# A hybrid encoder with normalised inputs: scale and offset applied per feature after the transpose, and a residual normed a second time

## The chip, the cores and the metric

The kernel runs on one core of a Trainium2 chip. The metric is device time in microseconds (us) of one execution of the program; lower is better. The engines are named as the profile names them: PE (TensorE matmul) and PEld (its weight loads), DVE (VectorE), ACT (ScalarE), POOL (GpSimd), SP (SyncE, which issues DMAs).

## The reference, cut to what matters

Sequence 256, width 2048, two layers, float32, one batch.

```python
x = layer_norm(x, ln_emb_g, ln_emb_b)
for l in range(2):
    u, g_ssm, q, k, v, g_attn = split(x @ w_in[l])        # w_in: 2048 x 6144
    y = ssm_d * u + s5_scan(forward) + s5_scan(reverse)   # 64 groups, 64 complex states
    y = gelu(y);  y = y * sigmoid(y @ w_glu[l] + b_glu);  y_ssm = y * silu(g_ssm)
    o = diff_attention(rotary(q), rotary(k), v, lam)      # 8 heads, two softmax maps each
    y_attn = rms_norm(o, attn_norm_g) * (1 - lambda_init) * silu(g_attn)
    x = layer_norm(ALPHA * x + concat(y_ssm, y_attn) @ w_out[l], ln_g[l], ln_b[l])
```

`layer_norm` works over the 2048 features of a token: `(x - mean) * rsqrt(var + eps) * g + b`, with `g` and `b` one number for each feature.

## The kernel before, in words

All large products run as three fp32r matmuls (`mm3`, L168 to L170): a number is split into a high part and a rest (`wh`/`wl` for weights, `xh`/`xl` for inputs, written hi and lo below), and hi·hi, hi·lo and lo·hi are added. Weights come from HBM in blocks of 512 rows by 256 columns (`load`, `raw`, L149, four buffers), each split by ACT (`wh`, L162) and DVE (`wl`, L164), two blocks ahead of their use. One block makes 24 matmuls of 256 columns.

A layer goes through: input projection (24 column blocks of four weight blocks), attention heads, the attention half of the output projection (8 column blocks `cb` of two weight blocks, L943 to L951), the GLU (L960 on), the other half of the output projection (L976 on), and the norm. The last column blocks of that half ("late") are computed for tokens 0 to 127 (`i=0`) and then for tokens 128 to 255 (`i=1`), so that the norm of `i=0` runs under the matmuls of `i=1`.

The norm, `ln_finish`, works on `r`, with tokens on partitions, in the memory of the tile `H` (which the scan uses between its start and `ssm_out`); `gt` and `bt`, also in `H`, hold `g` and `b` copied to all 128 partitions by broadcast loads (`load_gb`, 256 KB each). For a piece of `nk` blocks of 128 features it runs two DVE instructions:

```python
V.scalar_tensor_tensor(r[:, i, cs], r[:, i, cs], mv[:, 0:1], gt[:, cs], sub, mult)   # L229
last = V.scalar_tensor_tensor(r[:, i, cs], r[:, i, cs], rstd, bt[:, cs], mult, add)  # L235
```

then `trans` transposes it on PE (L248), ACT evicts the hi part (`xh`, L252) and DVE makes the lo part (`xl`, L253). `rstd` comes from two POOL instructions (L223 add, L224 power). The normed `r` is stored to `xres` in DRAM, and `xr` (L946, two buffers, shared with the attention's `q` and `k`) reads it back in the attention half of the output projection, where L951 makes `part_r = ALPHA * xr + acc`. The other half adds its sums to `part_r` into `r` (L985, L1007).

Side work (state tables, the scan's input, scan and output, heads, stores) is written as generators called lanes. After each weight block `side` gives them a budget of DVE time by their declared costs and gaps in steps, so the program order is fixed by that plan; `finish` runs a lane to its end. The compiler's scheduler then orders each engine's queue from this order with its own model of times: an instruction that it takes to be ready may stand ahead of earlier ones, loads above all. On the chip each queue is in order. `after(ins)` keeps an instruction behind `ins` in its queue.

Of the kernel before, what the change touches and what calls it, by code (L numbers as in the profile page):

```python
# [14 lines left out]
D = 2048  # L15
# [16 lines left out]
LAST_PIECES = (6,5,5)  # L32
# [7 lines left out]
HEAD_HOPS = (1,1,2,2,2,3)  # L40


@with_exitstack
def kernel(
# [45 lines left out]


# [14 lines left out]
    xv = x[0].rearrange("(k j) d -> j k d", j=4)  # L106
    ov = out[0].rearrange("(k j) d -> j k d", j=4)
# [33 lines left out]
    newest = [None]  # L141

    def load(i):
# [4 lines left out]
        raw = T([128, KT, 256], "raw", RAW_BUFS)  # L148
        newest[0] = SY.dma_start(  # L149
# [5 lines left out]
    def do_split(i, wh=None, wl=None, behind=None):  # L155
# [6 lines left out]
        A.copy(wh, raw)  # L162
        with after(behind):
            V.tensor_tensor(wl, raw, wh.bitcast(F32), sub)  # L164
# [35 lines left out]
    def ln_stats(r, i, c, st):  # L200
        V.bn_stats(st[:, i, c, :], r[:, i, c * 256:(c + 1) * 256])
# [3 lines left out]
    def store_x():  # L205
        yield 0.0, STORE_HOP
        n = 0
        while n < 9:
            if stores:
                SY.dma_start(*stores.pop(0))  # L210
                n += 1
            yield 0.0, 1

    def ln_finish(r, gt, bt, st, dst, box, ahead):


        pool = [None]

        def moments(i):
            mv = T([128, 2], "mv", 2)  # L220
            V.bn_aggr(mv, st[:, i].rearrange("p c s -> p (c s)"))
            rstd = T([128, 1], "rstd", 2)
            GP.tensor_scalar(rstd, mv[:, 1:2], EPS, None, add)  # L223
            pool[0] = GP.tensor_tensor(rstd, rstd, mhalf[:, 0:1], ALU.pow).ins  # L224
            return mv, rstd
# [5 lines left out]
        def norm(i, k0, nk, mv, rstd):  # L231
            cs = slice(k0 * 128, (k0 + nk) * 128)
            if dst is None or i == 0:
                centre(i, k0, nk, mv)
            last = V.scalar_tensor_tensor(r[:, i, cs], r[:, i, cs], rstd, bt[:, cs], mult, add)  # L235
            if dst is None:
                stores.append((xres[128 * i:128 * i + 128, cs], r[:, i, cs]))
            else:
                for j in range(2):
                    SY.dma_start(dst[2 * i + j][:, cs], r[64 * j:64 * j + 64, i, cs])  # L240
            return last.ins

        def trans(k0, nk, i0, ni):

            t = ss_bank([128, nk, 128 * ni])
            for k in range(nk):
                for i in range(ni):
# [829 lines left out]
```

## Time and profile before

| what | us |
|---|---|
| runs: median of 3 (lowest to highest) | 1003.33 (999.39 to 1005.35) |
| profiled execution, time | 1002.55 |
| profiled execution, span | 1000.8 |
| PE busy | 955.8 (96%) |
| DVE busy | 780.3 (78%) |
| ACT busy | 576.0 (58%) |
| POOL busy | 71.7 (7%) |

The span runs from the first to the last instruction; the execution's time is 1.75 us more. A busy time is the time in which an engine had at least one instruction in work; what PE lacks to the span is 45.0 us. DMA moved 177.76 MB, at a mean of 178 GB/s.

### The profile page before, as it was taken

What the parts mean: (1) busy time and instruction counts of PE and PEld (TensorE: products, weight loads), DVE (VectorE), ACT (ScalarE), POOL (GpSimd) and SP (SyncE); (2) the same over time, 40 slices, a digit from 0 to 9 for tenths busy, and PEclk for the clock granted to TensorE, in tenths of its full rate; (3) what the DMA queues carried; (4) which work ended last, traced back from release to release, by engine and by line L of the source; (5) the groups of instructions that cost most, each with busy time, mean ns of one, the idle gap of its engine ahead of it and who ended that gap; (6) DMA issues with size and microseconds to landing.
All of it is one profiled execution on the core that took longest, in us unless ns stands there. A gap on an engine that the chain in (4) does not pass through costs nothing.

```text
span 1000.8 us, 24625 instructions
## 1 busy us (share of the span) xinstructions
PE 955.8 (96%) x10304; PEld 926.8 (93%) x10304; DVE 780.3 (78%) x1353; ACT 576.0 (58%) x950; POOL 71.7 (7%) x103
## 2 busy tenths in 40 slices
PE   2999999999999998999979999999999999999995
PEld 2989988999999998999979989999999999999995
DVE  6875799899887786656588699899899759565676
ACT  2546588565575697545344585555556769843640
POOL 1000130210200000000011030010100100000001
PEclk9999999999999999999989999999999999999998
DMA  9898521545554643779875724555445454576953
GB/s 272 254 256 230 184 81 44 168 149 169 156 183 153 193 145 104 234 228 260 215 231 167 233 68 126 170 169 161 157 150 187 151 168 136 178 237 209 270 173 85
DMA packets 193167, 177.76 MB, mean 178 GB/s; under 512 B 37536, under 2 KB 185760, under 8 KB 193056
## 3 DMA queue, kind: packets, MB, share of 16 engines
q1 hardware_dynamic: 193056, 176.18, 58.7%
q8 instruction: 81, 1.33, 0.6%
q14 instruction: 30, 0.25, 0.1%
HBM read 165.02 MB, written 11.14 MB: 176 GB/s over the span
## 4 chain that ended last, share of the span: by engine, by line
PE 81%; DMA 7%; DVE 6%; ACT 3%; issue 1%; SPq 1%; POOL 0%; POOLq 0%; DVEq 0%; ACTq 0%
PE acc L168 23%; PE acc L169 23%; PE acc L170 23%; DMA raw<-in_w_out_dram 3%; PE ss L596 2%; DVE wl L164 2%; PE ss L501 1%; PE sc L707 1%; PE ss L735 1%; PE tp L473 1%; ACT wh L162 1%; PE tp L577 1%; DVE w L456 1%; DVE H L235 1%; DMA H<-in_x_dram 1%
## 5 line engine op out<-in xcount | busy, mean ns | idle before, releaser
L164 DVE TENSOR_TENSOR wl<-raw,wh 128x1024 fp32r<-128x1024 f32 x266 | 324.9, 1223 | 143.0 <-ACT wh L162 141.8
L162 ACT CAST wh<-raw 128x1024 fp32r<-128x1024 f32 x266 | 278.2, 1050 | 251.0 <-PE acc L169 118.7
L168 PE MATMUL acc<-xh,wh 128*128 128x256 f32 x1280 | 370.9, 290 | 0.8 <-ACT xh L252 0.5
L169 PE MATMUL acc<-xl,wh 128*128 128x256 f32 x1280 | 365.2, 286 | 0.8 <-DVE xl L253 0.7
L170 PE MATMUL acc<-xh,wl 128*128 128x256 f32 x1280 | 364.1, 285 | 1.1 <-DVE wl L164 1.1
L168 PEld LDWEIGHTS acc<-xh,wh 128*128 128x128 f32 x1280 | 245.5, 192 | 6.2 <-ACT xh L252 1.4
L169 PEld LDWEIGHTS acc<-xl,wh 128*128 128x128 f32 x1280 | 245.7, 192 | 2.4 <-DVE xl L253 1.5
L170 PEld LDWEIGHTS acc<-xh,wl 128*128 128x128 f32 x1280 | 245.6, 192 | 2.1 <-DVE wl L164 1.5
L168 PE MATMUL acc<-wh,xh 128*128 128x256 f32 x512 | 146.3, 286 | 0.0
L169 PE MATMUL acc<-wl,xh 128*128 128x256 f32 x512 | 145.4, 284 | 0.0
L170 PE MATMUL acc<-wh,xl 128*128 128x256 f32 x512 | 145.0, 283 | 0.0
L169 PEld LDWEIGHTS acc<-wl,xh 128*128 128x128 f32 x512 | 98.2, 192 | 0.2
L168 PEld LDWEIGHTS acc<-wh,xh 128*128 128x128 f32 x512 | 98.1, 192 | 0.1
L170 PEld LDWEIGHTS acc<-wh,xl 128*128 128x128 f32 x512 | 98.2, 192 | 0.0
L169 PE MATMUL acc<-wl,a 128*128 128x256 f32 x208 | 59.1, 286 | 2.1 <-DVE wl L164 2.1
L168 PE MATMUL acc<-wh,a 128*128 128x256 f32 x208 | 58.7, 284 | 0.0
L170 PE MATMUL acc<-wh,a 128*128 128x256 f32 x208 | 58.5, 283 | 0.0
L551 DVE TENSOR_TENSOR sa<-tab,H 128x256 f32<-128x256 f32 x126 | 53.0, 421 | 2.9 <-ACT H L504 0.7
L458 DVE TENSOR_TENSOR w<-w,x 128x512 f32<-128x512 f32 x64 | 45.6, 712 | 0.8
L169 PEld LDWEIGHTS acc<-wl,a 128*128 128x128 f32 x208 | 39.7, 191 | 3.3 <-DVE wl L164 3.3
L717 ACT ACTIVATE e<-sc,mx 128x256 f32<-128x256 f32 x64 | 29.5, 477 | 21.0 <-DVE mx L711 21.0
L168 PEld LDWEIGHTS acc<-wh,a 128*128 128x128 f32 x208 | 39.7, 191 | 0.4 <-ACT wh L162 0.4
(198 smaller groups left out, 1482.9 us busy)
## 6 DMA issues: line engine op xcount, KB each, us to landing
raw<-in_w_in_dram SPq DMA_DIRECT2D x192, 512.0 KB, 3.8
raw<-in_w_out_dram SPq DMA_DIRECT2D x64, 512.0 KB, 4.6
raw<-in_w_glu_dram SPq DMA_DIRECT2D x16, 512.0 KB, 4.4
xr<-xres SPq DMA_DIRECT2D x16, 256.0 KB, 4.3
xres<-H SPq DMA_DIRECT2D x14, 256.0 KB, 3.4
H<-in_x_dram SPq DMA_DIRECT2D x8, 256.0 KB, 5.9
u_dr<-ub SPq DMA_DIRECT2D x8, 256.0 KB, 3.3
a<-u_dr SPq DMA_DIRECT2D x8, 256.0 KB, 3.8
```

The costliest lines, as they stand in the source:

```text
L162: A.copy(wh, raw)
L164: V.tensor_tensor(wl, raw, wh.bitcast(F32), sub)
L168: PE.matmul(o, lhsT=lh, rhs=rh, start=first, stop=False, skip_group_check=True)
L169: PE.matmul(o, lhsT=lh, rhs=rl, start=False, stop=False, skip_group_check=True)
L170: PE.matmul(o, lhsT=ll, rhs=rh, start=False, stop=last, skip_group_check=True)
L235: last = V.scalar_tensor_tensor(r[:, i, cs], r[:, i, cs], rstd, bt[:, cs], mult, add)
L456: V.tensor_tensor(dst, t.unsqueeze(2).to_broadcast([128, 8, 16, 4]), M[:, m, gs, :].unsqueeze(3).to_broadcast([128, 8, 16, 4]), mult)
L458: V.tensor_tensor(w[:, r], w[:, r], x2, op)
L473: PE.transpose(t[:, pr, :], ws[o][:, ri, 2 * pr:2 * pr + 2].rearrange("p g c j -> p (g c j)"), ident)
L551: V.tensor_tensor(a.rearrange("p v q r g -> p v q (r g)"), lam, h.unsqueeze(1).to_broadcast([128, 2, 16, 8]), mult)
L596: PE.matmul(yps[d][halves[g2], pr, :], lhsT=w[halves[d], ri, g].rearrange("p c j -> p (c j)"), rhs=h[:, ::-1] if d else h, start=ri == 0, ...
L717: A.activation(e[:, m, i, :], sc[:, m, i, :], AF.Exp, bias=mx[:, c:c + 1], accum_out=sm[:, c:c + 1])
```

## The change

1. **Input norms** (`ln_in`). A piece is normed on tokens by one `tensor_scalar`, `(r - mean) * rstd`, into `xn` (the other half of the memory of `H`), and `r` stays as it was. After the transpose, features are on partitions, so `g` and `b` are one number for each partition: ACT evicts each block of 128 features with that scale and bias. At the first norm ("direct") ACT writes hi itself and DVE a full copy `hf`; at the second, ACT writes `hf` and then hi from it. The lo part is `hf - hi`. `g` and `b` come in as 32 rows and are turned by one PE transpose (`load_cols`, `cols`).
2. **Residual.** `xres` is not written for the first layer, and holds the un-normed `r` for the second. In the attention half of the output projection `xr` is loaded from `x` itself (first layer) or `xres`, normed with the kept mean and `rstd` and broadcast `gt`, `bt` (loaded there, 8 times 256 KB in a layer), and the sum goes straight into `r` in `H`; `part_r` is gone, and with it its hold on `xh1`, `xl1`, where the second half of the mixer's output now lies instead of in `a8`. `ssm_out` is finished before this part; the load and split of its result are a lane of their own (`ssm_y`).
3. **Start.** Ten matmuls on zeros ahead of everything on PE; `x` is loaded ahead of all weights, and the first weight load waits for the statistics of `i=0`.
4. **Small loads** (state tables, `ssm_d`, lambdas, `attn_norm_g`, `b_glu`) are kept behind the newest weight load, `lam_of` behind a weight split, and the table lane starts three steps later.
5. **`rstd`'s** addition moves from POOL to DVE. **Last norm** (`ln_out`): pieces of 6, 5, 3, 2 blocks instead of 6, 5, 5; stores go out on SP's and ACT's queues in turn.

```diff
-LAST_PIECES = (6,5,5)
+LAST_PIECES = (6,5,3,2)
+WARM = 10
+TAB_HOP = 3
...
-    def load(i):
+    def load(i, hold=None):
...
+        if hold is not None:
+            with after(hold):
+                V.memset(raw[:, 0, 0:1], 0.0)
...
-        r = h[:, 0:4096].rearrange("p (i d) -> p i d", i=2)
-        return r, h[:, 4096:6144], h[:, 6144:8192]
+        r, xn = [h[:, 4096 * n:4096 * n + 4096].rearrange("p (i d) -> p i d", i=2) for n in range(2)]
+        return r, xn
...
+        V.tensor_scalar(rstd, mv[:, 1:2], EPS, None, add)
+        pool = GP.tensor_tensor(rstd, rstd, mhalf[:, 0:1], ALU.pow).ins
...
+    def load_cols(gsrc, bsrc):
+        rows = T([32, 128], "on")
+        SY.dma_start(rows[0:16], gsrc.rearrange("(k p) -> k p", p=128))
+        SY.dma_start(rows[16:32], bsrc.rearrange("(k p) -> k p", p=128))
...
+    def cols(rows):
+        t = tp_bank([128, 32])
+        PE.transpose(t, rows, ident[0:32, 0:32])
+        gb = T([128, 32], "gb")
+        A.copy(gb, t)
...
+        def norm(i, k0, nk, m):
             cs = slice(k0 * 128, (k0 + nk) * 128)
+            return V.tensor_scalar(xn[:, i, cs], r[:, i, cs], m[0][:, 0:1], m[1], sub, mult).ins
...
-            A.copy(h, t)
-            V.tensor_tensor(lo_, t, h.bitcast(F32), sub)
+            hf = T([128, nk, 128 * ni], ("qs", "sh", "wT")[len(los) % 3])
+            for k in range(nk):
+                g, b = gb[:, k0 + k:k0 + k + 1], gb[:, 16 + k0 + k:17 + k0 + k]
+                if direct:
+                    last = A.activation(h[:, k], t[:, k], AF.Identity, bias=b, scale=g)
+                    V.tensor_scalar(hf[:, k], t[:, k], g, b, mult, add)
+                else:
+                    A.activation(hf[:, k], t[:, k], AF.Identity, bias=b, scale=g)
+            if not direct:
+                last = A.copy(h, hf)
+            box[2] = last.ins, V.tensor_tensor(lo_, hf, h.bitcast(F32), sub).ins
...
+            for j, eng in enumerate((SY, A)):
+                eng.dma_start(dst[2 * i + j][:, cs], r[64 * j:64 * j + 64, i, cs])
...
+    idle = tp_bank([128, 512])
+    for _ in range(WARM):
+        PE.matmul(idle, lhsT=zero[:, 0:128], rhs=zero, start=True, stop=True)
...
-        part_r = [T([128, D], tag) for tag in ("xh1", "xl1")]
+        finish(l_out)
+        r, xn = ln_tiles()
+        gt, bt = xn[:, 0], xn[:, 1]
+        g_, b_ = (ln_emb_g, ln_emb_b) if l == 0 else (ln_g[l - 1], ln_b[l - 1])
+        with after(newest[0]):
+            load_gb(gt, bt, g_, b_, slice(0, 512))
         for cb in range(8):
             cs = slice(cb * 256, (cb + 1) * 256)
             xr = T([128, 2, 256], "xr", 2)
-            SY.dma_start(xr, xres[:, cs].rearrange("(i p) d -> p i d", p=128))
+            if l == 0:
+                for j in range(2):
+                    SY.dma_start(xr[64 * j:64 * j + 64], xh_[j][:, :, cs])
+            else:
+                SY.dma_start(xr, xres[:, cs].rearrange("(i p) d -> p i d", p=128))
+            if cb % 2 == 0 and cb < 6:
+                with after(newest[0]):
+                    load_gb(gt, bt, g_, b_, slice(256 * cb + 512, 256 * cb + 1024))
...
             for i in range(2):
-                V.scalar_tensor_tensor(part_r[i][:, cs], xr[:, i], ALPHA, acc[:, i, :], mult, add)
-        finish(l_out)
+                mv, rstd, _ = box[3][i]
+                V.scalar_tensor_tensor(xr[:, i], xr[:, i], mv[:, 0:1], gt[:, cs], sub, mult)
+                V.scalar_tensor_tensor(xr[:, i], xr[:, i], rstd, bt[:, cs], mult, add)
+            V.scalar_tensor_tensor(r[:, :, cs], xr, ALPHA, acc, mult, add)
+        finish(l_y)
...
-        M.h.append(T([128, 8, 256], "a8", 3, F32R))
-        M.l.append(T([128, 8, 256], "a8", 3, F32R))
+        M.more()
...
-            with after(newest[0]):
-                load_gb(gt, bt, ln_g[l], ln_b[l], slice(512 * b, 512 * b + 512))
+            if l + 1 == DEPTH:
+                with after(newest[0]):
+                    load_gb(gt, bt, ln_g[l], ln_b[l], slice(512 * b, 512 * b + 512))
```

## Rows read from the trace of the kernel before

**Rows 1.** The page's busy time, share of the span and instructions of each engine

```profile
PE 955.8 (96%) x10304; PEld 926.8 (93%) x10304; DVE 780.3 (78%) x1353; ACT 576.0 (58%) x950; POOL 71.7 (7%) x103
```

**Rows 2.** Busy time by stretch: length, engines' us (instructions), granted clock, DMA share, GB/s

```profile
0.00:20.00 20.00, 1.80 (x6) 1.01 (x6) 10.39 (x25) 3.19 (x5) 3.69 (x12) 1.00 0.92 265
20.00:60.00 40.00, 38.27 (x291) 36.32 (x292) 36.38 (x82) 19.54 (x29) 0.00 (x0) 1.00 0.86 256
...
380.00:400.00 20.00, 17.15 (x342) 16.43 (x338) 12.16 (x19) 15.26 (x29) 0.00 (x0) 0.91 0.33 100
...
480.00:500.00 20.00, 19.10 (x152) 18.10 (x150) 12.35 (x21) 7.25 (x7) 0.00 (x0) 1.00 0.86 222
500.00:520.00 20.00, 15.28 (x120) 14.33 (x120) 17.28 (x30) 8.19 (x11) 2.54 (x4) 0.96 0.71 219
520.00:540.00 20.00, 18.89 (x142) 18.52 (x143) 18.89 (x29) 8.56 (x13) 0.84 (x1) 0.87 0.63 194
```

**Rows 3.** Timeline of the start: start, us, engine, line, [idle before, releaser]

```profile
5.53 1.41 DVE L201 BATCH_NORM_STATS2 st<-H 128x6 f32<-128x256 f32 x4 [5.53 <-DMA H<-in_x_dram]
...
14.89 1.40 DVE L201 BATCH_NORM_STATS2 st<-H 128x6 f32<-128x256 f32 x4 [0.94 <-DMA H<-in_x_dram]
...
21.24 0.41 PE L170 MATMUL acc<-xh,wl 128*128 128x256 f32 x1
```

**Rows 4.** Timeline of PE: an attention product whose operands are plain float32

```profile
302.32 1.05 PE L735 MATMUL ss<-v,wT 128*128 128x128 f32 x8
```

**Rows 5.** Timeline of DVE, then of PE, at the hoisted lambda loads

```profile
317.28 0.29 DVE L663 TENSOR_TENSOR on<-on 128x128 f32<-128x128 f32 x1 [4.16 <-DMA on<-in_lambda_k_dram]
319.29 0.39 PE L170 MATMUL acc<-xh,wl 128*128 128x256 f32 x1 [1.08 <-DVE wl L164]
```

**Rows 6.** Timelines of SP, DVE and PE where layer 2 begins

```profile
514.21 1.12 SPq L427 DMA_DIRECT2D a<-in_ssm_c_re_dram  x2
...
519.76 0.48 DVE L235 SCALAR_TENSOR_TENSOR H<-H,rstd 128x256 f32<-128x256 f32 x1 [0.47 <-POOL rstd L224]
...
521.02 1.94 PE L446 MATMUL tp<-cst,a 128*128 128x128 f32 x8 [4.31 <-DMA a<-in_ssm_c_re_dram]
...
523.91 0.80 PE L168 MATMUL acc<-xh,wh 128*128 128x256 f32 x2
```

**Rows 7.** Groups by line and shape: count, busy us, mean ns of one, idle before

```profile
L229 DVE SCALAR_TENSOR_TENSOR H<-H,mv 128x512 f32<-128x512 f32 x18 | 13.4, 746 | 0.1
L316 DVE TENSOR_SCALAR kx<-kx 128x128 f32<-128x128 f32 x1 | 0.2, 218 | 0.0
L253 DVE TENSOR_TENSOR xl<-ss,xh 128x512 fp32r<-128x512 f32 x14 | 9.5, 682 | 0.9 <-ACT xh L252 0.7
L162 ACT CAST wh<-raw 128x1024 fp32r<-128x1024 f32 x266 | 278.2, 1050 | 251.0 <-PE acc L169 118.7 <-PE acc L170 92.2 <-DMA raw<-in_w_out_dram 13.6
L967 ACT ACTIVATE sh<-acc,bg 128x256 f32<-128x256 f32 x8 | 3.4, 470 | 0.0
L969 ACT CAST a<-sh 128x512 fp32r<-128x512 f32 x4 | 2.5, 621 | 0.0
```

**Rows 8.** Second layer's attention half of the output projection: DVE, SP, DVE; landing of `xr`

```profile
885.33 0.42 DVE L951 SCALAR_TENSOR_TENSOR xh<-xr,acc 128x256 f32<-128x256 f32 x1 [0.57 <-PE acc L170]
...
886.11 0.37 SPq L946 DMA_DIRECT2D xr<-xres  x1
...
889.29 1.23 DVE L164 TENSOR_TENSOR wl<-raw,wh 128x1024 fp32r<-128x1024 f32 x1 [1.65 <-ACT wh L162]
891.09 0.42 DVE L951 SCALAR_TENSOR_TENSOR xh<-xr,acc 128x256 f32<-128x256 f32 x1 [0.58 <-PE acc L170]
...
DMA to landing us min/median/max: 3.6/3.7/4.7
```

**Rows 9.** Timeline of the end: POOL and SP

```profile
990.50 1.04 POOL L223 TENSOR_SCALAR rstd<-mv 128x1 f32<-128x1 f32 x1 [7.36 <-DVE mv L221]
993.78 3.98 SPq L240 DMA_DIRECT2D out_dram<-H  x6
```

More of the change, by code (lines that the diff above doesn't have):

```diff
@@ L161, in do_split @@
             wl = T([128, KT, 256], "wl", SPLIT_AHEAD + 1, F32R)
-        A.copy(wh, raw)
-        with after(behind):
-            V.tensor_tensor(wl, raw, wh.bitcast(F32), sub)
+        with after(behind[0]):
+            newest[2] = A.copy(wh, raw).ins
+        with after(behind[1]):
+            newest[1] = V.tensor_tensor(wl, raw, wh.bitcast(F32), sub).ins
         split[i] = (wh, wl)
@@ L206, in store_x @@
         yield 0.0, STORE_HOP
[L207 to L211, printed above, removed]
-            yield 0.0, 1
[L214 to L225, printed above, removed]
+        while stores:
+            SY.dma_start(*stores.pop(0))
+            yield 0.0, 1
@@ L255, in ln_finish @@
-        mv, rstd = moments(0)
-        if dst is None:
-            box[0] = Pair()
-        m0 = mv, rstd
-        last = None
-        for k0 in range(0, ahead, 4):
-            nk = min(ahead - k0, 4)
-            with after(last if k0 else None):
-                last = norm(0, k0, nk, *m0)
-            if dst is None:
-                trans(k0, nk, 0, 1)
-        yield
-        mv, rstd = moments(1)
-        if dst is None:
-            box[0].more()
-        if dst is not None:
-            k0 = k1 = 0
-            for nk in LAST_PIECES + (0,):
-                if nk:
-                    with after(last):
-                        centre(1, k0, nk, mv)
-                if k0:
-                    last = norm(1, k1, k0 - k1, mv, rstd)
-                k0, k1 = k0 + nk, k0
-            return
@@ new lines, in norm @@
+            return last.ins
+        mv, rstd, _ = moments(st, 0)
+        last = None
+        for k0 in range(0, 16, 4):
+            with after(last):
+                centre(0, k0, 4, mv)
+                last = norm(0, k0, 4, mv, rstd)
+        yield
+        mv, rstd, _ = moments(st, 1)
+        k0 = k1 = 0
+        for nk in LAST_PIECES + (0,):
+            if nk:
+                with after(last):
+                    centre(1, k0, nk, mv)
+            if k0:
+                last = norm(1, k1, k0 - k1, mv, rstd)
+            k0, k1 = k0 + nk, k0
@@ L808 @@
             SY.dma_start(cst[:, 0:C_SEL], consts[:, 0:C_SEL])
[L809 to L814 removed]
+            rows = load_cols(ln_emb_g, ln_emb_b)
+    idle = tp_bank([128, 512])
+    for _ in range(WARM):
+        PE.matmul(idle, lhsT=zero[:, 0:128], rhs=zero, start=True, stop=True)
+    gb = cols(rows)
     st = T([128, 2, 8, 6], "st")
     box = {}
[L817 to L822 removed]
+    ln = ln_in(r, xn, gb, st, box, 4)
+    for c in range(8):
+        seen = ln_stats(r, 0, c, st)
+    for c in range(RAW_BUFS):
+        load(c, hold=seen if c == 0 else None)
+    SY.dma_start(cst[:, C_SEL:], consts[:, C_SEL:])
+    next(ln)
+    for c in range(8):
+        ln_stats(r, 1, c, st)
     for i in range(SPLIT_AHEAD):
         next(ln)
[L825 removed]
+        do_split(i, behind=box[2] if i else (box[4], box[2][1]))
         load(RAW_BUFS + i)
@@ L1006 @@
                 cs = slice(cb * 256, (cb + 1) * 256)
-                V.tensor_tensor(r[:, i, cs], part_r[i][:, cs], accs[n][:, i], add)
+                V.tensor_tensor(r[:, i, cs], r[:, i, cs], accs[n][:, i], add)
                 ln_stats(r, i, cb, st)
+            if l + 1 < DEPTH:
+                stores.extend((xres[128 * i:128 * i + 128, c:c + 1024], r[:, i, c:c + 1024]) for c in (0, 1024))
             do_split(ji + 2 * len(late) + i)
```

156 lines of the change are left out of this document (91 added, 65 removed).

## The prediction

> **What bounds the kernel now.** I read the busy times of the page first, then busy time by stretch, then the timelines of the stretches where PE is not full, then durations by shape. PE is busy 955.8 us [rows 1], so of the profiled execution's 1002.55 us only 45 us of its span and 1.75 us around it are not PE work. The change adds and removes next to no PE work, so it can only move those 45 us, or open new gaps. The view by stretch [rows 2] shows where they lie: 18.2 us in the first 20 us, 1.7 in the next 40, 2.9 between 380 and 400, 0.9, 4.7 and 1.1 in the three stretches from 480 to 540, where the granted clock is also below full, and the rest, some 12 us, behind the last matmul. PE being the bound almost everywhere, added work on DVE or ACT costs nothing while it stays inside a weight block's 2.88 us (half of the 5.76 us between the two L951 of neighbouring column blocks [rows 8]); that is the first thing to test for each edit.
>
> **Start.** The first steady matmul is at 21.24; the last piece of `x` came at 14.89, the first, of 512 KB, at 5.53 [rows 3]. In these 20 us the DMAs ran at 265 GB/s [rows 2], shared by `x`, the weights and 2 MB of broadcast `g` and `b`. The change takes the broadcasts out and holds the weights back, so the other 1.5 MB of `x` need 5.9 us behind 5.53: 11.4. From the last landing to the steady matmul it was 6.35 us. There POOL's addition, 0.7 to 1.0 us (one of 1.04 in [rows 9]), becomes a DVE instruction of at most the 0.22 of a `tensor_scalar` [rows 7]; against that hi now takes two evictions where there was one, and lo waits for `hf`: about 0.5 more. So 6.2, and a start at 17.6: 3.6 us gained. Bounds: nothing, if `x` comes no earlier or PE is not free, and 6.
>
> PE's freedom is the zeros' matter. A float32 product of 128 columns shows as two instructions, eight in 1.05 us [rows 4], so at most 0.13 each. Ten of 512 columns are 80 such, 8 to 10.5 us at full clock (2.4 GHz), 16 to 21 at half (1.2). From 2 us on, with the first part at half clock, that ends near 14, ahead of the second half's transposes. I take nothing for a warmer clock: in [rows 2] the mean is down to 0.96 and 0.87 around the wait at 517, so an idle stretch of that kind gives the clock back, and PE will wait here again.
>
> **Ramp, 20 to 60 us.** DVE is busy 36.4 of 40 us [rows 2]. Four feature blocks of both token halves, used up by two weight blocks (5.76 us), cost DVE four 746 ns instructions, two 682 ns and two splits of 1.23 [rows 7, 8]: 6.8 us, more than PE takes. After, two `tensor_scalar` replace the four. No row has one of 512 columns. It is at most the 746 of the two-operand form, and at least the 218 of one of 128 columns; I take 500, since the form at 128 columns is short and most of 512 is stream. Then 4.8 us, under 5.76. Of the 1.7 us of PE gaps I take 0.7 back (0 to 1.7). Gone besides are the first layer's `xres` stores (2 MB), and the table, lambda and gain loads wait behind weights.
>
> **ACT in the same ramp.** For two feature blocks it had one eviction; now two with 256 columns and a copy of 512. The nearest eviction, with one per-partition operand, takes 470 ns, the copy 621, a weight split 1050 [rows 7]; two weight blocks then come to 4 x 0.47 + 2 x 0.62 + 2.1 = 5.2 of 5.76 us. It is hidden, but by little. The Trainium skill's page "ScalarE: Activation LUTs", section "What ACT_TABLE_LOAD costs", says that each per-partition pointer operand adds about 93 ns to an ACTIVATE; here scale and bias both are such, and no row has two. By it the sum is 5.6 of 5.76 us, still hidden, but each layer's first matmul comes some 0.2 us later, and my total would be 0.4 us higher.
>
> **Lambda loads.** The second layer's were put so early that DVE stood 4.16 us on them and PE 1.08 [rows 5]. Held behind weights and used a column block later, they have landed: 1.1 us gained (0 to 1.1). The three steps by which the table lane starts later cost nothing: by the lanes' gaps it ends at step 21 instead of 18, and the scan's input waits for the parameter load, which ends at step 25 in both.
>
> **Start of layer 2.** PE stood 4.31 us on a load of `ssm_c` issued at 514.21 [rows 6], the moment a buffer of `a8` came free: two of three held the mixer's second half until its last matmul. Now that half lies in `xh1`, `xl1`, so the load can go out from the GLU's end on. What is late next is the norm of `i=1`. It was ready at 519.76 + 0.48 = 520.24; ahead of it DVE loses four 746 ns instructions and gains two of 500 for `i=0`, and POOL's addition goes: about 2 us earlier, 518.3. Transposes take 0.6, two evictions and a copy, of 128 and 256 columns, some 1.1, against 0.4 before. So the matmul of 523.91 [rows 6] starts at 520.2: 3.7 us gained (0 to 5). In the first layer's GLU 2 MB of broadcasts go, while 1 MB of `ssm_c` comes forward into the same stretch; of the 0.9 us lost to weights between 480 and 500 [rows 2] I take 0.5 back, bounds a loss of 2 and all 0.9.
>
> **Residual.** For each column block L951's two instructions of 0.42 become four and one of 512 columns: 4 x 0.45 + 0.75 = 2.55 against 0.85, so 1.7 us more on DVE, 27 us for the 16. What hides it is the idle time there: two splits of 1.23 and the 0.85 leave 2.5 of 5.76 us free [rows 8], now 0.8. `ssm_out` is done by then anyway, since by the lanes' plan its last step falls three weight blocks ahead of this part, in both kernels, so `finish` there adds no wait, and the load and split of its result keep their steps; I leave the gap at 383 as it is. Broadcasts add 2 MB to 46 us whose load in the first layer is near what the DMAs gave at the start; weights are four blocks ahead there. For small waits on DVE I add 0.5 us a layer, 1 in all; the bounds are nothing and the first rival's price.
>
> **End.** POOL's 1.04 becomes 0.22: 0.8 gained. The extra piece costs about 0.2. Six stores took 3.98 us of SP's queue, 0.66 each [rows 9]; two queues take one issue off the end, and the last piece is 256 columns instead of 640. I take 1.3 (0.5 to 2).
>
> **Sum.** 3.6 + 0.7 + 1.1 + 3.7 + 0.5 + 1.3 - 1.0 = 9.9 us. 1002.55 - 9.9 = 992.6, against a median of 1003.33 for the runs shown, 0.8 above the profiled execution. A difference of 0.5%, 5 us, is about what a measurement here can tell.
>
> **Rivals.**
>
> *DVE stands on `xr`* (the slower side). `xr` has two buffers, so the load for block cb+2 leaves when the sum of cb is done (issued at 886.11) and lands 3.7 us later in the median [rows 8]. Before, nothing used it for another 7 us. Now its four norm instructions are ready for the scheduler the moment it takes the load to have landed, and [rows 5, 6] show that it takes loads to be faster than they are. If they are queued ahead of the second split of the block (889.29, 3.2 us behind the sum), split and sum stand behind them: 3.7 + 1.9 + 1.2 + 0.75 = 7.6 us for a block instead of 5.76. Six blocks of a layer lose 1.8 each, 11 us, less some 3 that PE has in hand: 8 a layer, 11 in the first if its load takes 4.2. Then 1002.55 - 10.9 + 19 = 1010.7. It decides as soon as the landing passes 1.9 us with that order; queued behind the second split, landings up to 4 us cost nothing. Against it: the split and the sum are earlier in program order, and the window for an early place is short.
>
> *The gains are hidden.* The zeros hold PE to 20 us, or the `ssm_c` load does not move because `a8` is handed out in order and the new `U` takes the place: without these two, 1002.55 - 2.6 = 1000.
>
> *The gap at 383 goes too.* PE lost 2.9 us there and some at a clock of 0.91 [rows 2], behind ACT's GELU. As a lane of its own, its place in ACT's queue may differ: 992.6 - 4 = 988.6.
>
> **Numbers.** Forecast 0.60, alone 985 to 998; `xr` 0.15, of which a third hits one layer only and ends near 1000; hidden gains 0.15; the gap gone too 0.10. The range 984 to 1006 leaves out the full `xr` case and little below. Faster by over 0.5%: 0.57 of the forecast, 0.10, 0.04 of the hidden gains: 0.71. Within 0.5%: 0.03 + 0.10 + 0.05 = 0.18. Slower: 0.11.
>
> **What would show it.** First steady matmul near 17.6, with `x` landed by 11.4; no wait of DVE on lambdas; the first matmul of layer 2 some 3.7 us after the last of layer 1, with `ssm_c` landed long before; PE full through both attention halves of the output projection, and no idle of DVE ended by `xr`. Wrong would be: PE below full there, DVE's idle time ended by DMA, or ACT as the releaser of PE in either ramp.

## The result, and the profile after

The changed kernel is slower: 1015.0 us (median of 4 runs, 1013.04 to 1015.78) against 1004.34 us (median of 4 runs of the kernel before beside them), a ratio of 1.0121 with a 95% interval of 1.0096 to 1.0147. Forecast were 992.6 us, between 984 and 1006. The profiled execution took 1014.34 us, with a span of 1012.5.

The page's busy times, and busy time by stretch of the changed kernel (columns as in [rows 2]):

```profile
PE 965.6 (95%) x10326; PEld 930.9 (92%) x10326; DVE 794.8 (78%) x1389; ACT 591.1 (58%) x991; POOL 63.3 (6%) x98
```

```profile
0.00:20.00 20.00, 11.95 (x27) 5.21 (x27) 10.09 (x30) 4.33 (x9) 2.83 (x11) 0.90 0.82 229
20.00:60.00 40.00, 37.33 (x277) 35.22 (x278) 31.33 (x68) 25.51 (x41) 0.00 (x0) 0.92 0.52 160
140.00:180.00 40.00, 35.02 (x806) 31.11 (x805) 36.84 (x62) 31.27 (x56) 6.75 (x12) 1.00 0.14 42
380.00:400.00 20.00, 13.73 (x306) 12.59 (x307) 13.02 (x24) 13.43 (x27) 0.00 (x0) 0.95 0.52 148
400.00:450.00 50.00, 47.66 (x392) 46.69 (x388) 36.31 (x52) 21.37 (x25) 0.00 (x0) 0.98 0.68 205
480.00:500.00 20.00, 20.00 (x169) 20.00 (x168) 14.54 (x20) 7.33 (x7) 0.00 (x0) 1.00 1.09 301
500.00:520.00 20.00, 19.53 (x165) 19.33 (x164) 15.08 (x25) 8.68 (x11) 0.56 (x1) 1.00 0.78 253
520.00:540.00 20.00, 16.54 (x131) 15.23 (x132) 19.20 (x33) 17.21 (x37) 5.62 (x5) 1.00 0.27 83
880.00:920.00 40.00, 34.48 (x273) 33.53 (x272) 27.66 (x44) 12.45 (x12) 0.00 (x0) 0.96 0.78 235
```

Three stretches of the kernel before that [rows 2] does not have, in the same view:

```profile
140.00:180.00 40.00, 38.70 (x734) 34.36 (x728) 36.42 (x65) 29.65 (x58) 9.29 (x12) 1.00 0.17 47
400.00:450.00 50.00, 50.00 (x419) 49.89 (x418) 30.08 (x38) 23.47 (x26) 0.00 (x0) 1.00 0.74 232
880.00:920.00 40.00, 40.00 (x336) 40.00 (x335) 22.64 (x30) 14.34 (x15) 0.00 (x0) 1.00 0.73 229
```

The zeros count as PE work, so the sum of busy time hides where time went. It is read from marks that both programs have (start of the same ACT or DVE instruction; after minus before):

| mark | before | after | shift | forecast of the step |
|---|---|---|---|---|
| first input block evicted | 50.1 | 52.2 | +2.1 | -4.3 (start, ramp) |
| last gate ahead of the output projection | 392.6 | 393.4 | +0.8 | -1.1 (lambdas) |
| last sum of layer 1's attention half | 441.2 | 450.1 | +8.8 | +0.5 |
| end of the GLU | 464.4 | 472.7 | +8.3 | |
| first input block of layer 2 | 550.9 | 553.0 | +2.1 | -4.2 (start of layer 2, `w_out`) |
| last gate of layer 2 | 876.1 | 879.2 | +3.2 | |
| last sum of layer 2's attention half | 920.2 | 932.3 | +12.1 | +0.5 |
| end of the span | 1000.8 | 1012.5 | +11.7 | -1.3 (end, from +12.4 at the end of the GLU) |

So the two attention halves cost 8.0 and 8.9 us (from the last gate to the last sum), the start is 6.4 us behind its forecast, and the start of layer 2 gained 6.2, more than forecast. The gap at 383 did not go: between 380 and 400 us PE lacks 6.3 us instead of 2.9.

What ended VectorE's idle time, of the changed kernel's view of waits (us in total, times, longest):

```profile
DVE xr L1024 <- DMA xr<-in_x_dram: 8.7, 3, 4.2
DVE xr L1024 <- DMA xr<-xres: 8.6, 3, 4.9
...
DVE xr L1024 <- issue: 6.0, 2, 5.5
DVE xr L1024 <- DMA H<-in_ln_emb_g_dram: 2.2, 1, 2.2
```

25.5 us on the residual's norms, 6.0 of them without a releaser that the profile shows; the longest of these, 5.5, ends at 897.82, 5.8 us after the load of that block left. PE stands behind VectorE there. What ended its idle time from 880 to 933 us:

```profile
PE acc L176 <- DVE H L1026: 3.7, 2, 2.2
PE acc L177 <- DVE wl L172: 1.9, 3, 1.5
```

In the place of [rows 8], the timelines of DVE and then SP:

```profile
891.08 1.22 DVE L172 TENSOR_TENSOR wl<-raw,wh 128x1024 fp32r<-128x1024 f32 x1
897.82 0.88 DVE L1024 SCALAR_TENSOR_TENSOR xr<-xr,mv,H 128x256 f32<-128x256 f32 x2 [5.53 <-issue]
898.62 1.22 DVE L172 TENSOR_TENSOR wl<-raw,wh 128x1024 fp32r<-128x1024 f32 x1
...
901.34 0.68 DVE L1026 SCALAR_TENSOR_TENSOR H<-xr,acc 128x512 f32<-128x512 f32 x1
...
907.39 2.35 DVE L172 TENSOR_TENSOR wl<-raw,wh 128x1024 fp32r<-128x1024 f32 x2
914.66 0.88 DVE L1024 SCALAR_TENSOR_TENSOR xr<-xr,mv,H 128x256 f32<-128x256 f32 x2 [4.92 <-DMA xr<-xres]
```

```profile
891.99 0.39 SPq L1015 DMA_DIRECT2D xr<-xres  x1
892.47 7.77 SPq L156 DMA_DIRECT2D raw<-in_w_out_dram  x2
```

The norm of a later block (L1024) waits for its load, and the split of a weight block (898.62) stands behind it. While that split is late no `raw` buffer comes free, so the next weight load sits on SP's queue, 7.77 us for two (the second leaves at 899.87, where the split ends), and whatever is queued behind it sits too.

The start, in the place of [rows 3]: timelines of DVE, then ACT, then PE.

```profile
12.69 1.41 DVE L209 BATCH_NORM_STATS2 st<-H 128x6 f32<-128x256 f32 x4 [0.24 <-DMA H<-in_x_dram]
...
15.68 0.40 DVE L265 TENSOR_SCALAR qs<-ss,gb 128x128 f32<-128x128 f32 x1
17.04 0.41 DVE L265 TENSOR_SCALAR sh<-ss,gb 128x128 f32<-128x128 f32 x1 [0.96 <-ACT xh L264]
```

```profile
16.55 1.75 ACT L264 ACTIVATE xh<-ss,gb 128x128 fp32r<-128x128 f32 x4 [2.48 <-PE ss L256]
19.20 0.46 ACT L264 ACTIVATE xh<-ss,gb 128x128 fp32r<-128x128 f32 x1 [0.91 <-DVE qs L265]
19.56 1.03 ACT L170 CAST wh<-raw 128x1024 fp32r<-128x1024 f32 x1
```

```profile
20.65 0.58 PE L176 MATMUL acc<-xh,wh 128*128 128x256 f32 x1 [4.14 <-ACT wh L170]
...
23.64 0.41 PE L176 MATMUL acc<-xh,wh 128*128 128x256 f32 x1
```

`x` is there at 12.7 (forecast 11.4), the steady matmul comes at 23.6 (forecast 17.6). ACT and DVE evict the same PSUM tile, one waiting for the other, and ACT's first weight split comes behind all of it. The spacing of the matmuls falls from 0.21 to 0.12 us only at 26.7; before, at 24.1.

Where layer 2 begins, in the place of [rows 6] (SP, PE):

```profile
472.84 1.53 SPq L470 DMA_DIRECT2D a<-in_ssm_c_re_dram  x2
```

```profile
522.08 0.71 PE L464 MATMUL tp<-cst,a 128*128 128x128 f32 x4 [2.55 <-ACT bh L465]
...
525.69 0.48 PE L176 MATMUL acc<-xh,wh 128*128 128x256 f32 x2
```

`ssm_c` leaves 41 us earlier and nothing waits for it.

### The profile page after: what moved, and what is told of

The parts are those of the page before. It is cut to its first block, busy times and chain, and to the rows that moved or that the text cites. A ratio compares the mean times of both kernels' runs of the same rounds, so it can differ in the third digit from the quotient of the medians.

```text
span 1012.5 us, 24767 instructions
## 1 busy us (share of the span) xinstructions
PE 965.6 (95%) x10326; PEld 930.9 (92%) x10326; DVE 794.8 (78%) x1389; ACT 591.1 (58%) x991; POOL 63.3 (6%) x98
## 2 busy tenths in 40 slices
DMA packets 191569, 175.71 MB, mean 174 GB/s; under 512 B 37536, under 2 KB 185568, under 8 KB 191456
## 4 chain that ended last, share of the span: by engine, by line
PE 75%; DVE 11%; DMA 6%; ACT 4%; issue 2%; SPq 1%; POOL 0%; DVEq 0%; ACTq 0%
PE acc L176 22%; PE acc L177 21%; PE acc L178 21%; DVE wl L172 2%; PE ss L640 2%; DMA raw<-in_w_out_dram 2%; DMA xr<-xres 1%; PE ss L787 1%; DVE w L500 1%; PE sc L759 1%; DMA xr<-in_x_dram 1%; DVE x L500 1%; DVE w L502 1%; ACT wh L170 1%; PE ss L545 1%
## 5 line engine op out<-in xcount | busy, mean ns | idle before, releaser
L177 PE MATMUL acc<-wl,xh 128*128 128x256 f32 x720 | 206.0, 287 | 4.4 <-DVE wl L172 4.3
L176 PE MATMUL acc<-wh,xh 128*128 128x256 f32 x720 | 205.9, 286 | 3.7 <-DVE H L1026 3.7
L178 PE MATMUL acc<-wh,xl 128*128 128x256 f32 x720 | 205.0, 285 | 0.0
L177 PEld LDWEIGHTS acc<-wl,xh 128*128 128x128 f32 x720 | 139.2, 194 | 6.0 <-DVE wl L172 5.9
L176 PEld LDWEIGHTS acc<-wh,xh 128*128 128x128 f32 x720 | 139.3, 194 | 4.1 <-issue 4.0
L178 PEld LDWEIGHTS acc<-wh,xl 128*128 128x128 f32 x720 | 139.4, 194 | 0.1
L598 DVE TENSOR_TENSOR H<-sa 128x128 f32<-128x128 f32 x126 | 36.1, 287 | 2.1
L597 DVE TENSOR_TENSOR sa<-sa,H 128x128 f32<-128x128 f32 x126 | 36.2, 287 | 2.0
L548 ACT COPY H<-ss 128x512 f32<-128x512 f32 x32 | 34.0, 1175 | 5.2 <-PE ss L545 5.2
L178 PE MATMUL acc<-bh,wl 128*128 128x256 f32 x128 | 36.2, 283 | 0.0
```

The source lines that it names most:

```text
L176: PE.matmul(o, lhsT=lh, rhs=rh, start=first, stop=False, skip_group_check=True)
L177: PE.matmul(o, lhsT=lh, rhs=rl, start=False, stop=False, skip_group_check=True)
L178: PE.matmul(o, lhsT=ll, rhs=rh, start=False, stop=last, skip_group_check=True)
L548: A.copy(z.H[:, 2 * o:2 * o + 2, 1:65].rearrange("p q k r g -> p q (r g) k")[:, :, g2::2], ps[g2].rearrange("p q r g k -> p q (r g) k"))
L597: V.tensor_tensor(a[:, 0], a[:, 0], nx, add)
L598: V.tensor_tensor(nx, a[:, 0], a[:, 1, :, ::-1, :], add)
```

## The experiments

All comparisons are with the kernel before, run beside the changed one on the same chip. The chip is not the same for all experiments, so what one run gains over another is read from their ratios: a thousandth is about 1 us. Each edit is against the changed kernel unless the text says otherwise.

### The residual: order, places, or work

**Norms kept behind a split.**

```diff
-            for s in (0, 1):
-                sub_step(acc, s, M.hi, M.lo, 0, 7, tok_major=True)
+            sub_step(acc, 0, M.hi, M.lo, 0, 7, tok_major=True)
+            first = newest[1]
+            sub_step(acc, 1, M.hi, M.lo, 0, 7, tok_major=True)
...
+                with after(first):
                     V.scalar_tensor_tensor(xr[:, i], xr[:, i], mv[:, 0:1], gt[:, cs], sub, mult)
```

> The four norm instructions of a column block are only kept behind the split of that block's first weight block on VectorE; nothing else changes, no buffer is added, every load leaves as before. Theory (VectorE stands on xr: norms queued ahead of a split and a sum): the two attention halves, which came 8.0 us (layer 1) and 9.2 us (layer 2) later against before, give back most of it, because a load that lands 2.7 to 7.9 us after the sum of the block two before now has about 7 us: 1015 - 15 = 1000 us, VectorE's waits on xr under 4 us. Rival A (VectorE is simply too full, 2.55 us of new work in a block of 5.76): no wait is taken away, 1013 to 1016. Rival B (the loads themselves are slow because two broadcasts and the weights share the DMAs): the norms wait at their new place as well, about 1008.

Measured 1005.2 us, ratio 1.0036 [1.0016, 1.0055]. An order edge, and no other change, gives back 8.5 us of the 12.1 that the change had lost by the ratios. Against rival A. VectorE still stands 9.7 us on `xr`, where the theory had under 4, so rival B is true in part.

**A place for each block.** `xr` in `xh1`, `xl1`; `SY.dma_start` of block `cb` where it was, held behind the newest weight load.

> xr gets a place of its own for each of the eight column blocks (in the two buffers that the normed residual had in the kernel before), so that no load waits for a sum; order of the norms left to the scheduler. Theory (the wait is the load that leaves only at a sum): loads leave two blocks or more earlier, 1015 - 15 = 1000 us, as in the run with the norms kept behind the split. Rival A (VectorE too full): 1013 to 1016. Rival B (slow loads): eight loads of 256 KB early beside weights take the DMAs, PE waits for weights instead, 1006 to 1012.

1013.0 us, 1.011 [1.0078, 1.0142]: nothing, and the theory as put there (the load leaves only at a sum) is wrong. VectorE's waits on the loads rose from 23 to 32 us.

**No norm.** The four norm instructions are left out, so the residual is not normed.

> The two norm passes of the residual are left out: the sum takes the loaded xr as it is, so the output is that of an un-normed residual. Loads, broadcasts and buffers stay. Theory (wait by order): the sum is the only user of xr, it stands two blocks behind the start of the load, so nothing waits: 1015 - 17 = 998 us; and the run that only keeps the norms late comes within 2 us of it. Rival A (VectorE too full): also 998, but then the run with late norms stays near 1015. Rival B (slow loads): sums wait for landings over 8 us, none seen, 998 to 1000.

1000.1 us, 0.9984 [0.9967, 1.0001]: 13.7 us come from the norms, by their order or by their work.

**Loads two blocks ahead**, with a place for each block; first with the scheduler's order, then with the late norms.

```diff
+        for cb in range(AHEAD):
+            load_xr(cb)
         for cb in range(8):
...
+            if cb + AHEAD < 8:
+                load_xr(cb + AHEAD)
```

> xr has a place of its own for each column block, and each load is put two blocks ahead of its use in the order of the program, so ahead of the weight loads of those blocks on SP's queue; the order of VectorE is the scheduler's, as in the changed kernel. What the run with places alone left open: its loads stood on SP's queue behind a weight load that waited for a raw buffer, which a split frees that stands on VectorE behind the norms that wait for xr. Theory (that ring): now nothing in it waits; 1015 - 13 = 1002 us, VectorE's waits on xr under 4 us. Rival A (VectorE too full): waits of VectorE on DMA go, PE still stands behind VectorE's splits and sums, 1008 or more. Rival B (DMAs near their limit in this stretch): landings stay at 6 us and more, weights come late instead, 1006 to 1012.

> The loads two blocks ahead in places of their own, and the norms kept behind the split of the block's first weight block as in the run that did only this. Theory: both holes are closed, so it is the faster of the two or equal to it: 1001 us, within 2 us of the run without the norms (1000.1). Rival A (VectorE's 1.7 us a block more do not fit beside the splits): 1004 or more, PE's waits ended by VectorE without a wait of VectorE on DMA. Rival B (DMAs at their limit): weights late, 1004 to 1010.

1018.25 us, 1.0169 [1.0145, 1.0192], and 1008.25 us, 1.0064 [1.0043, 1.0084]. Both theories missed. Earlier loads brought nothing either time: 4.8 us more than the changed kernel, and 2.8 more than the late norms alone, where the intervals overlap. DVE in the run without late norms:

```profile
399.75 0.88 DVE L1035 SCALAR_TENSOR_TENSOR xh<-xh,mv,H 128x256 f32<-128x256 f32 x2 [4.32 <-DMA xh<-in_x_dram]
...
402.24 0.87 DVE L1035 SCALAR_TENSOR_TENSOR xh<-xh,mv,H 128x256 f32<-128x256 f32 x2
...
406.15 1.22 DVE L173 TENSOR_TENSOR wl<-raw,wh 128x1024 fp32r<-128x1024 f32 x1
```

With loads that the scheduler takes to be early, it puts the norms of three blocks ahead of the split that PE needs. A buffer doesn't help against an order that follows it. The order is the cause; more room only moves the norms forward.

**Norms one place later**, behind the split of the second weight block, alone:

> The changed kernel with the norms kept behind the split of the second weight block, and nothing else. Theory (the order is the larger part of what the residual cost): 1015 - 11 = 1004 us, 1 us below the run with the first place (1005.2). Rival (the gain of the run with start and order came from the start): 1010 and more.

1005.3 us, 1.0035 [1.0018, 1.0051]: the same as the first place, 8.6 us back, not 11. DVE there, second layer:

```profile
894.67 1.22 DVE L172 TENSOR_TENSOR wl<-raw,wh 128x1024 fp32r<-128x1024 f32 x1
895.80 0.87 DVE L1026 SCALAR_TENSOR_TENSOR xr<-xr,mv,H 128x256 f32<-128x256 f32 x2
896.60 0.88 DVE L1027 SCALAR_TENSOR_TENSOR xr<-xr,rstd,H 128x256 f32<-128x256 f32 x2
897.39 1.22 DVE L172 TENSOR_TENSOR wl<-raw,wh 128x1024 fp32r<-128x1024 f32 x1
898.52 0.68 DVE L1028 SCALAR_TENSOR_TENSOR H<-xr,acc 128x512 f32<-128x512 f32 x1
```

Split, norm, split and sum stand behind each other with no gap, 4.5 us from 894.67 on, inside a block of 5.76 us.

**Norms on GpSimd.**

```diff
-                V.scalar_tensor_tensor(xr[:, i], xr[:, i], mv[:, 0:1], gt[:, cs], sub, mult)
-                V.scalar_tensor_tensor(xr[:, i], xr[:, i], rstd, bt[:, cs], mult, add)
+                GP.tensor_scalar(xr[:, i], xr[:, i], mv[:, 0:1], rstd, sub, mult)
+            GP.tensor_tensor(xr, xr, gt[:, cs].unsqueeze(1).to_broadcast([128, 2, 256]), mult)
+            GP.tensor_tensor(xr, xr, bt[:, cs].unsqueeze(1).to_broadcast([128, 2, 256]), add)
```

> The second norm is taken from VectorE and done by GpSimd (two tensor_scalar of 256 columns, a product and a sum of 512 columns per column block), all else as in the changed kernel. Theory (what costs is that the norms stand in VectorE's queue ahead of splits and sums): GpSimd has no split in its queue, a late load delays only its own block, whose sum is not due for another block; if its four instructions stay under 5.76 us a block (estimate 5.4, from its copies of 256 columns at 0.9 us) the time is 1015 - 13 = 1002 us, near the run without norms (1000.1). Rival (VectorE's sums still wait on GpSimd, which is too slow): over 5.76 us a block, each us above costs 8 us a layer; at 8 us a block 1015 + 18 = 1033. Rival (the ring is in the loads): as the changed kernel, 1013 to 1016.

1031.3 us, 1.03 [1.0273, 1.0327]. The rival: GpSimd is too slow, and VectorE's sums stand 18.9 us on it. Groups of POOL (count, busy, mean ns):

```profile
L1024 POOL TENSOR_SCALAR xr<-xr,mv,rstd 128x256 f32<-128x256 f32 x32 | 51.6, 1619 | 70.1 <-DMA xr<-in_x_dram 35.6 <-DVE wl L172 24.0 <-DMA xr<-xres 10.3
L1026 POOL TENSOR_TENSOR xr<-xr,H 128x512 f32<-128x512 f32 x16 | 25.2, 1588 | 0.3
L1025 POOL TENSOR_TENSOR xr<-xr,H 128x512 f32<-128x512 f32 x16 | 24.3, 1532 | 175.8 <-DMA H<-in_ln_g_dram 91.2 <-DMA H<-in_ln_emb_g_dram 84.3
```

2 x 1.62 + 1.59 + 1.53 = 6.4 us a block, over 5.76, and the loads' wait comes on top.

### The start

**VectorE alone evicts**, ACT copies hi in SBUF; then **no zeros** (`WARM = 0`); then both.

```diff
                 if direct:
-                    last = A.activation(h[:, k], t[:, k], AF.Identity, bias=b, scale=g)
                     V.tensor_scalar(hf[:, k], t[:, k], g, b, mult, add)
...
-            if not direct:
-                last = A.copy(h, hf)
+            last = A.copy(h, hf)
```

> In the first norm alone the f32 tile is evicted by VectorE and ScalarE copies hi from it in SBUF, so the two engines no longer read one PSUM tile in turn. Theory (the alternation of the two evictions holds the first matmul: 1.0 + 0.9 + 0.5 us of waits between them): first steady matmul at about 21.5 instead of 23.3, 1015 - 1.7 = 1013.3 us. Rival (the start hangs on stats, norm and transposes, or on the weights' split that is kept behind): 23.3 stays, 1015; or, as the copy follows the eviction instead of running beside it, 0.5 us later.

> The changed kernel without the ten products of zeros at the start. Theory (the zeros buy nothing, as PE stands from 13.5 to 20.6 us behind them and goes on at half clock up to 26): same time, 1013 to 1016, first steady matmul within 0.5 us of 23.3, half clock behind it for about 3 us as in the kernel before. Rival (they hold back the first transposes, which were ready at 11.1 and ran at 12.85): up to 1.5 us faster, 1013. Rival (they keep the clock up): 2 us slower, 1017.

> The changed kernel with the first norm's tiles evicted by VectorE alone and no zeros, and nothing else. Theory (the alternating evictions cost what the forecast of the start missed, some 4 us at the end of the first input blocks): 1015 - 4 = 1011 us. Rival (each of the two alone gave nothing, so both together give nothing here, and the 4 us between the runs with loads ahead came from elsewhere): 1014 to 1016.

1013.6 us, 1.0119 [1.0077, 1.0161]; 1015.9 us, 1.0138 [1.0099, 1.0176]; both together 1012.3 us, 1.009 [1.0067, 1.0112]. The eviction was the hold: in the run with it and the zeros the first input block ends at 46.2 us, 3.9 ahead of the kernel before. There the profiled run lost it again: ACT stood 9.4 us on `raw` between 55 and 80 us, with DMAs busy, as the rival in its expectation had it. Without the zeros it ends at 46.9, and the last gate ahead of the output projection comes at 388.9, 3.7 us ahead. The first matmul is not what counts: with no zeros and both engines evicting, the steady matmul comes at 21.67, 2.0 us earlier than in the changed kernel, and the first input block ends at 53.3 all the same. For the run with both edits, DVE, then PE:

```profile
13.93 1.35 DVE L264 TENSOR_SCALAR qs<-ss,gb 128x128 f32<-128x128 f32 x4
```

```profile
18.98 0.58 PE L176 MATMUL acc<-xh,wh 128*128 128x256 f32 x1 [0.83 <-ACT xh L267]
```

Four evictions in 1.35 us, none waiting.

### The rest of the change alone

The kernel before with the lambdas later, the residual's sums in `H` (so that `a8` is free), the addition for `rstd` on VectorE, and more pieces and two queues at the end; normed rows are stored and read as before.

> The kernel before with the rest of the change alone: lambdas loaded and used later, the sums of the residual in the scan's memory so that the mixer's second half goes to the place of the hidden layer's and a8 comes free, the addition of epsilon on VectorE, last stores in more pieces and over two queues. Not in it: the norm by transposed columns, the second norm in the output projection, the zeros; the normed rows are stored and loaded as before. Theory (these steps of the forecast hold and do not hang on the two others): about 4 us at the start of layer 2, 1 for the lambdas, 1 at the end: 1002 - 6 = 996 us. Rival (the shorter start of layer 2 comes from the norm without gain and offset on the rows, not from the memory): 999 to 1000. Rival (waiting for the scan's output before the attention half costs as much as the memory gives): 1002 and more.

1006.8 us, 1.0045 [1.0029, 1.0061]: slower than before. The shift is +4.9 us at the first input block (a weight split of ACT stood 6.3 us behind the row norms of DVE, a new order there), +4.1 at the first block of layer 2 and +2.7 at the end of the span. Behind that loss, which no step of the forecast is about, the run gains 2.2 us, 0.8 of them from the GLU to layer 2. The wait for `ssm_c` is gone: the last matmul of layer 1 and the first of layer 2 are 6.9 us apart, 9.8 before:

```profile
520.67 0.36 PE L171 MATMUL acc<-bh,xl 128*128 128x256 f32 x1
...
527.55 0.50 PE L169 MATMUL acc<-xh,wh 128*128 128x256 f32 x2 [0.46 <-ACT xh L253]
```

Most of these 2.9 us were lost ahead of it (busy time by stretch of this run, the end of the GLU and what follows):

```profile
465.00:500.00 35.00, 31.86 (x250) 31.32 (x249) 19.90 (x26) 12.59 (x15) 0.00 (x0) 0.95 0.99 270
```

PE stands 3.1 us, on ACT's weight splits, where it stood 0.9 before. The DMA share is 0.99, as the loads of `ssm_c` now meet the weights and 2 MB of broadcasts. But in the changed kernel, without the broadcasts, the share from 480 to 500 is 1.09 and PE is full, so a busy DMA alone does not explain the wait. Two issues of `ssm_c` hold SP's queue for 7.2 us here (one for 4.6 in the changed kernel), with the weight loads behind them; whether the broadcasts make that difference is not shown.

### Towards a better version

**Norm on GpSimd with the start's edits**; **loads ahead, norms late, start's edits**; **second place and start's edits**.

> The norm on GpSimd, and at the start the eviction by VectorE alone with hi copied in SBUF and no zeros. Theory (the two are independent, and the start's edit gives what it gave between the runs with loads ahead and late norms, 4.4 us): 4 us below the run with the norm on GpSimd alone, 998 us. Rival (the start's gain is given back where weights come late between 60 and 75 us): within 1 us of it.

> The loads two blocks ahead, the norms late, the first norm evicted by VectorE alone with hi copied in SBUF, and no zeros. Theory (start and attention half are independent): what the two residual edits give, 1001, less 1 to 2 for the start: 999.5 us. Rival (the start's gain is given back between 60 and 75 us, where the weights come late behind the scatter of u, as in the run with that start alone): 1001.

> The norms kept behind the split of the second weight block of their column block (one place later than in the first run of this kind), two buffers for xr and the loads as in the changed kernel, and the start's edit. Theory (order alone): landings of up to 8 us fit, so the 3 to 4 us that still stood in the first run go: 1005 - 4.4 - 2 = 998.5 us. Rival (there VectorE is late with the sum instead, as 1.8 us of norms now stand between split and sum): 1001 and more, PE waiting for an accumulator that a sum holds.

1021.4 us, 1.02 [1.0168, 1.0231]; 1003.5 us, 1.0024 [1.0005, 1.0042]; and 999.8 us, 0.9966 [0.9949, 0.9984], faster than both kernels. The first two missed their theories. With the runs of each part alone: order 0.9 points off the ratio, start 0.3, both 1.55. That is 0.4 more than the sum, and the intervals of the four runs together are as wide, so it may be nothing. Between runs that differ in the start's edits alone these gave 0.3, 0.4, 0.7 and 1.0 points.

**Lambdas in another place**, on top of that:

```diff
-        t = T([128, 4, 64], "on")
+        t = T([128, 4, 64], "e4")
```

> The best so far (norms behind the second split, start's edit) with one more edit: the lambdas are loaded into the place of the attention's exponentials instead of the small buffer `on`. Theory (in the changed kernel the loads hold `on` from 79 to 118 us, so the table's last pieces, which go through the same buffer, come at 120 instead of 90 us, the scan's input begins at 131 instead of 117 us, meets the rotary and the first heads, and PE stands 5.0 us between 140 and 180 instead of 1.3): `on` pieces at about 90, PE's idle time between 120 and 180 back to 1.5 us, 999.8 - 3 = 996.8 us. Rival (the 5 us belong to the lane's later start, three steps, whatever `on` does): within 1 us of 999.8.

998.15 us, 0.9961 [0.9942, 0.998]. The wait is real: ACT's last pieces of the tables, in the changed kernel and in this run, and this run's stretch from 140 to 180:

```profile
120.07 0.21 ACT L426 COPY on<-tp 128x64 f32<-128x64 f32 x1
```

```profile
89.12 0.21 ACT L424 COPY on<-tp 128x64 f32<-128x64 f32 x1
```

```profile
140.00:180.00 40.00, 38.68 (x668) 34.96 (x666) 35.80 (x65) 30.22 (x59) 8.25 (x11) 1.00 0.20 59
```

The pieces are back at 89 to 93, PE's idle time is back to 1.3 us. But 0.9961 and 0.9966 can't be told apart: what it is worth stays open, between nothing and some 2 us.

**Zeros again**, and **VectorE's eviction at layer 2 as well**, each on top of the run with the lambdas' place:

> The same with the ten products of zeros again. Theory (zeros only bridge 2 to 14 us; PE stands behind them and starts at half clock in either case): same time as without, within 1.5 us. Rival (with them the first input blocks end 2 us earlier, 46.2 instead of 48.3, as in the run with VectorE's eviction and zeros, and that holds to the end): 2 us faster. Rival (then the weights come late behind the scatter of u, between 60 and 75 us): 2 to 4 us slower.

> The same as the run with the lambdas' own place, and VectorE instead of ScalarE evicts the first two groups of four feature blocks of token half 0 at the start of layer 2. Theory (ScalarE's evictions of 128 columns, 0.46 us each, hold the transposes of the scan's B and of the norm there: PE stands 2.6 + 0.4 + 0.7 us between 515 and 523): 1 to 2 us faster than without. Rival (VectorE has the norms of i=1 and the scan's tables there, and is as full as ScalarE): same or slower by 1.

999.2 us, 0.9976 [0.9957, 0.9995], and 999.5 us, 0.9968 [0.9951, 0.9985]. Neither differs from the run without it. So at layer 2, where ACT alone evicted, VectorE's eviction gives nothing, as the rival had it.

**The same without the two norm passes** (un-normed residual):

> The run with the lambdas' own place without the two norm passes of the residual (the sum takes the loaded xr as it is). It says what the norms still cost where their order is right. Theory (VectorE's 1.8 us a block nearly fit): 996 us, within 2.5 us of the run with them (998.2). Rival (they are most of what is left): 992 or less.

994.5 us, 0.9917 [0.9899, 0.9936]: 4.4 us is what the norms' work costs where their order is right (5.1 without the start's edits, 1.0035 against 0.9984). Neither bound was met.

## Why the prediction was wrong

**Residual: the step that failed.** The work was sized rightly (four instructions of 0.48, one of 0.68 us), and the wrong sentence is "For small waits on DVE I add 0.5 us a layer". The first rival came true, with its mechanism and nearly its price: 8.0 and 8.9 us measured, 11 and 8 forecast for it. What speaks for it is not two traces alone: the order by itself gives 8.6 us back, more buffers and earlier loads nothing or less. From the last gate to the end of the GLU the two layers take 71.8 and 67.3 us in the kernel before, 79.3 and 76.5 in the changed one, 75.3 and 68.9 with the norms behind the second split, and 73.0 and 67.4 without the norms. The rival's condition, that the norms get queued ahead of the second split, was given a chance of 0.15 on the ground that split and sum are earlier in program order; but the text had already said that the scheduler takes loads to be faster than they are [rows 5, 6]. Two things were missing in it. The norms of the first block wait for a broadcast as well (2.2 us at 392 us, ahead of `ssm_out`'s last work, where PE then stood 2.15 us on `ub`), and a late split holds the `raw` buffers and so SP's queue. Beyond the order, 1.7 us more in each block were costed at nothing, since they fit the idle time: 4.4 us in all were measured.

**Start: mis-sized at one term, for the most part.** `x` came 1.3 us later than forecast. "About 0.5 more" for two evictions in the place of one was some 5 us by the end of the first input block: it ends between 51.4 and 53.3 us in the nine profiled runs where both engines evict, and between 46.1 and 48.3 in the nine where VectorE does alone, with the zeros or without. That is 1.8 to 4.0 earlier than before, against the 4.3 forecast. At the steady matmul half of it shows: 10.9 us behind the last landing instead of 6.2, and 8.3 with VectorE evicting alone (12.61 to 20.95). The Trainium skill's page "PSUM — Partial Sum Buffer", section "PSUM bank collisions raise a hardware error", says that the compiler's scheduler adds a dependency between two instructions of different engines on one bank and quadrant, reads too. The waits of 0.96 and 0.91 us between L264 and L265, which have only the tile `ss` and the read `gb` in common, agree, and the rule would have shown this at the diff. The zeros were read rightly as worth nothing by themselves.

**Table lane: "cost nothing" missed a buffer.** The forecast looked at the lanes' steps and not at the buffers: the lambdas now hold the small buffer `on` from 79 to 118 us, through which the tables' last pieces go. The scan's input begins at 131 us instead of 117, and PE stands 5.0 us between 140 and 180 instead of 1.3. The lambda wait of [rows 5] did go. From the first input block to the last gate the change took 1.3 us less all the same, near the 1.1 forecast for the lambdas; what made good the 3.7 us was not looked for.

**Start of layer 2: right, and under-sized.** The gap between PE's last matmul of layer 1 and the first of layer 2 went from 9.8 to 6.4 us, 3.4 for a forecast of 3.7. By stretch, PE's idle time from 480 to 540 us fell from 6.7 us [rows 2] to 3.9, and the granted clock, 0.96 and 0.87 from 500 to 540 behind PE's wait, is now 1.00, by an estimate worth 20 x 0.04 + 20 x 0.13 = 3.4 us: 2.8 + 3.4 is the 6.2 of the marks, and the sum had left the clock out. The reason given holds for the gap: with the memory alone it is 6.9 us, so 2.9 of the 3.4 come with it. That run lost most of this again on weights ahead of the gap and kept 0.8; which of the lighter norm and the missing broadcasts spares the changed kernel that loss was not tried.

**ACT and end.** ACT's evictions with two per-partition operands took 0.57 to 0.62 us for 256 columns where one operand takes 0.47. The Trainium skill's page "ScalarE: Activation LUTs", section "What ACT_TABLE_LOAD costs", states 93 ns for each such operand; 0.10 to 0.16 was measured. At the start of layer 2 eight evictions of 128 columns, 3.0 us, stood ahead of `bh` on ACT, and ACT was the releaser of PE (2.55 us on `bh`), which the forecast had named as a sign of being wrong. The end gained 0.7 of 1.3.

**The sum.** The best run that computes the whole result is at 0.9961, some 4 us below the kernel before instead of 9.9. Without the norms' work it is 0.9917, 994.5 us beside a median of 1001.3: some 8.3 of the 10.9 us that the forecast had as gains exist. What stood against them was, by the runs, where the scheduler put four instructions a block (8.6 us), the work of these four (4.4), and the two evicting engines at the start (3 us by the run with the start's edits alone).

## What to carry to other kernels

When an edit makes an instruction depend on a load alone, ask where the scheduler will queue it: one that is "ready" early goes ahead of work that the bound engine needs, so tie it by an order edge behind that work, and only then give the load more room. Look through every small buffer that a moved load now holds for longer, for its other users. Let one engine evict a PSUM tile and make the second copy from SBUF.

## What the runs showed that was not expected

- GpSimd and VectorE were slower beside each other, in the run with the norms on GpSimd: a product of 512 columns took GpSimd 1.29 us in some places and up to 2.26 in others, and VectorE's product of 2048 columns 2.78 us in the mean instead of 2.28 in the changed kernel. The two such products: 2.29 us with GpSimd idle (from 891.54), 3.27 with GpSimd busy throughout (from 415.72). No run here shows why. Single splits took up to 2.33 instead of 1.22, this one beside a product of GpSimd:

```profile
429.78 1.30 POOL L1025 TENSOR_TENSOR xr<-xr,H 128x512 f32<-128x512 f32 x1
429.82 2.33 DVE L172 TENSOR_TENSOR wl<-raw,wh 128x1024 fp32r<-128x1024 f32 x1 [1.22 <-ACT wh L170]
```

- The clock at the start: with the zeros busy from 2.3 to 12.7 us and PE mostly idle behind them, the granted clock was 0.50 (1.2 GHz) from 16 to 26 us. The records of the kernel before give 1.00 in all of its start, though its matmuls are 0.21 us apart up to 24.1 us and 0.12 after, and so do those of the changed kernel without zeros: here, behind a long idle time, the spacing says more than the record.
- Loads sent two blocks earlier made the changed kernel 4.8 us slower, with no more bytes moved (175.71 MB in both).
